# One pool for MLP and embedding, an early load of p, and w1's products sorted into high and low runs

## The chip, the cores and the metric
The kernel runs on one core of a Trainium2 chip. The metric is the device time of one execution in microseconds. Engines are named as the profile names them: PE is TensorE's matmul, PEld its weight load, DVE is VectorE, ACT is ScalarE, SP is SyncE, which issues most of the DMAs. L173 is line 173 of the kernel before.

## The reference
A trunk of two layers over 256 tokens of width 2048, in float32. Each layer adds three terms to h:

```
h += mixer(rmsnorm(h))                     # layer 0: RG-LRU; layer 1: 2-D neighbourhood attention
h += relu(rmsnorm(h) @ w1)^2 @ w2          # w1: 2048 x 8192, w2: 8192 x 2048
h += sigmoid(rmsnorm(h) @ Wg) * (p @ Wp)   # Wg: 2048 x 2048, p: 256 x 256, Wp: 256 x 2048
```

A last rmsnorm ends it. The third line is called the embedding here; Wg is `ple` and Wp is `proj` in the kernel.

## The kernel before
Every operand of a product is split into a high part, rounded to the format in which TensorE multiplies (fp32r), and a low part, the rest. A product is high x high + high x low + low x high, all summed in PSUM.

**Weights.** `block` (L93) loads 1 MB of weights into a buffer `raw` (SP, L98) and splits it in two halves: a cast to `wh` on ACT (L105) and a subtraction to `wl` on DVE (L106). A half is a step, and covers two rows of 128 inputs by 512 outputs. There are three raw buffers for the whole kernel and four `wh` and four `wl`; a stage may add raw buffers of its own from its pool (`phase`, L87): two in the MLP and two in the embedding, none in the mixers. The buffers are used in turn.

**Two ways to multiply.** `tproduct` (L136: w2, the output products, the gate) keeps the activations stationary and streams 512 columns of weights, eight matmuls with `wh` (L143, L144) and then four with `wl` (L148) for each step. `add` (L159: w1, and q and k of the attention) keeps a 128 x 128 piece of the weights stationary. For each of four output tiles and each of two rows it issues the high product with 512 columns (L173: the high and the low half of the activations side by side) and then the low product with 256 columns (L174), which is added to the second half of the same PSUM tile. A group is 8 steps x 4 tiles x 2 rows = 64 such pairs. The first two steps of a group are done first for tiles 0 and 1, then for tiles 2 and 3 (`held`, L176 to 187). In the mixer of layer 0, w_in goes through `product` (L189), three matmuls of 256 columns.

PSUM has three accumulators `mm` of two tiles each; a group of `add` takes two. `joined` (L201) adds the two halves of a PSUM tile: ACT copies the second half (L204), DVE adds (L206), after which the accumulator is free.

**MLP** (L581). It has a pool of its own, with the tile r2 (the squared norm factor) and the two raw buffers. For each quarter f: four groups of w1, each squared and split into activations, then four products with w2, each of eight steps and summed into h by `residual_add` (L339, L346 with r2 as the factor). In the last quarter the sum is followed by `settle` (L284): the squares of h on ACT (L222), then transposes and the split for the next stage.

**Embedding** (L612). A new pool, opened when the MLP's has been closed. `ple_load` loads p from ACT's queue (L608) and splits it (L198, L199) into `pls`. Then for each of four groups: twelve matmuls of p with proj (L636 to 638), and the gate, a product by `tproduct` of eight steps, with sigmoid and sum.

**Order.** The tile framework places instructions in each engine's queue by order of the program and by when it reckons them ready, and adds the waits. A tile of a new pool waits for the tiles of the closed pool whose place it takes. `self.later` holds small pieces of work that `tick` (L117) advances once after every step.

Of the kernel before, what the change touches and what calls it, by code (L numbers as in the profile page):

```python
# [19 lines left out]
P = 128  # L20
D = 2048
T = 256
# [8 lines left out]
V_MIX, V_MLP, V_PLE, V_FIN, V_CW, V_CB, V_AB, V_XB, V_LAM = 0, 2, 4, 6, 7, 11, 12, 14, 16  # L31
# [7 lines left out]
class Late:  # L39


    def __init__(self, tiles):
        self.tiles = tiles
# [8 lines left out]
class Trunk:  # L52
    def __init__(self, ctx, tc, d):
        self.tc, self.nc, self.d = tc, tc.nc, d
        nc = self.nc
        pool = lambda name, bufs, **kw: ctx.enter_context(tc.tile_pool(name=name, bufs=bufs, **kw))
        self.const = pool("const", 1)
        self.state = pool("state", 1)
        self.wraw = pool("wraw", 3)
        self.wsplit = pool("wsplit", 4)  # L60
        self.work = pool("work", 2)
        self.psum = pool("psum", 3, space=PSUM)
        self.psm = pool("psm", 2, space=PSUM)

        self.vec = self.const.tile([P, N_VEC * NC], F32, name="vec")
        self.ones = self.const.tile([P, P], F32, name="ones")
        self.ident = self.const.tile([P, P], F32, name="ident")
        nc.gpsimd.memset(self.ones, 1.0)
        make_identity(nc, self.ident)
        nc.scalar.dma_start(self.vec, d["vec"])  # L70
        self.later = []
        self.spare, self.turn = (None, 0), 2
        self.ahead = 0

    def v(self, which, c):
        i = which * NC + c
        return self.vec[:, i : i + 1]
# [81 lines left out]
    def add(self, ps, w, xs, quarters, before=None, loads=1, summed=False):  # L159
        nc = self.nc  # L160

        def tiles(step, ts):
            k0, wh, wl = step
            for t in ts:
                o = ps[t // 2][:, t % 2, :]
                c = slice(t * P, (t + 1) * P)
                for k in range(2):
                    kc = k0 + k
                    first, last = kc == 0, kc == len(xs) - 1
                    if summed:  # L170
                        self.product(o, wh[:, k, c], wl[:, k, c], xs[kc], first, last)
                    else:
                        nc.tensor.matmul(o, wh[:, k, c], xs[kc], start=first, stop=False)  # L173
                        nc.tensor.matmul(o[:, T:], wl[:, k, c], xs[kc][:, :T], start=False, stop=last)  # L174

        held = []  # L176
        for step in self.steps(w, quarters, loads):
            if before:
                before(step[0])
            if step[0] < 4:  # L180
                tiles(step, (0, 1))
                held.append(step)
                if len(held) == 2:
                    for s in held:
                        tiles(s, (2, 3))
            else:
                tiles(step, range(4))
# [390 lines left out]
        return out  # L578


    def mlp(self, layer, home, other):  # L581

        with self.phase("mlp", 2) as pool:
            self._mlp(pool, layer, home, other)

    def _mlp(self, pool, layer, home, other):
        nc = self.nc
        r2 = pool.tile([P, 2], F32, name="r2")
        self.norm_later(lambda r: nc.vector.tensor_tensor(r2, r, r, ALU.mult))
        xs = self.xlist(self.xs)  # L590
        for f in range(4):
            acts = []
            for g in range(4):
                ps = self.group(self.d["w1"][layer, 4 * f + g], xs)
                o = self.state.tile([P, 4, 512], F32R, name=f"{other}{g}")
                for i in range(2):
                    u = self.joined(ps[i], "u")
                    nc.vector.scalar_tensor_tensor(u, u, 0.0, u, ALU.max, ALU.mult)
                    self.split(o[:, 2 * i : 2 * i + 2, :], u)
                acts.append(o)  # L600
            w = lambda g: self.d["w2"][layer, g, 4 * f : 4 * f + 4]
            self.residual(w, self.xlist(acts), V_PLE + layer, home, by=r2, last=f == 3)


    def ple_load(self, pool, layer):
        nc = self.nc
        raw = pool.tile([P, 2, T], F32, name="p_raw")
        nc.scalar.dma_start(raw, self.d["p"][layer])  # L608
        self.pls = pool.tile([P, 2, 512], F32R, name="pls")
        self.split(self.pls, raw)  # L610

    def ple(self, layer, which, home):  # L612
        with self.phase("ple", 2) as pool:
            self.ple_load(pool, layer)
            self._ple(pool, layer, which, home)

    def _ple(self, pool, layer, which, home):
        nc = self.nc
        r = pool.tile([P, 2], F32, name="r_ple")
        self.norm_later(lambda tok: nc.vector.tensor_copy(r, tok))  # L620
        xs = self.xlist(self.xs)
        if which is not None:
            self.xs = self.new_xs(home)
        else:
            gain = pool.tile([P, D], F32, name="gain")
            nc.scalar.dma_start(gain, self.d["gain"])
        for g in range(NG):
            if g % 2 == 0:
                halves = self.block(self.d["proj"][layer, g // 2])
            wh, wl = (t.rearrange("p (k n) -> p k n", k=2) for t in next(halves))  # L630
            pj = pool.tile([P, 2, 512], F32, name="pj", bufs=2)
            pp = [self.psm.tile([P, 512], F32, name="pp", tag="psm") for _ in range(2)]
            for s in range(2):
                for k in range(2):
                    xh, xl = (self.pls[:, k, a + s * P : a + (s + 1) * P] for a in (0, T))
                    nc.tensor.matmul(pp[s], xh, wh[:, k, :], start=k == 0, stop=False)  # L636
                    nc.tensor.matmul(pp[s], xl, wh[:, k, :], start=False, stop=False)
                    nc.tensor.matmul(pp[s], xh, wl[:, k, :], start=False, stop=k == 1)
                nc.scalar.copy(pj[:, s, :], pp[s])
            ps = self.tgroup(self.d["ple"][layer, g], xs)  # L640
            if g == 0:
                self.norm_begin()
            for s in range(2):
                h = self.h[g][:, s, :]
                u = self.work.tile([P, 512], F32, name="u", tag="joined")
                nc.scalar.activation(u, ps[:, s, :], AF.Sigmoid, scale=r[:, s : s + 1])
                nc.vector.tensor_tensor(u, u, pj[:, s, :], ALU.mult)
                nc.vector.tensor_tensor(h, h, u, ALU.add)
                if which is None:
                    self.norm_square(g, s)  # L650
                    nc.vector.tensor_tensor(h, h, gain[:, 512 * g : 512 * (g + 1)], ALU.mult)
            if which is not None:
                self.settle(g, which, self.xs[g])
        if which is None:
            self.last()
# [15 lines left out]
    def run(self):  # L671
        self.load_h()
        self.rg_mixer()
        self.mlp(0, "xs", "as")
        self.ple(0, V_MIX + 1, "as")
        self.na_mixer()
        self.mlp(1, "as", "xs")
        self.ple(1, None, None)

# [79 lines left out]
```

## Time and profile before

| | us |
|---|---|
| median of 3 runs | 2383.24 |
| the three runs | 2381.78, 2383.24, 10307.08 |
| profiled execution | 2382.47 |
| its span | 2380.7 |
| PE busy | 2330.8 (98%) |
| PEld busy | 1996.5 (84%) |
| DVE busy | 1422.3 (60%) |
| ACT busy | 1177.4 (49%) |

The span is the time from the first to the last instruction of the profiled execution. Busy times of engines lie beside each other. A matmul's listed duration overlaps with the next matmul's; how fast TensorE works is read from the distance of the starts. The mean granted clock of TensorE is 0.993 of full speed. The chain that ended last runs over PE for 92% of the span. One of the three runs is far off the others; the profile agrees with those two.

### The profile page before, as it was taken

To read this page: it belongs to the slowest core of one execution; us is meant where nothing else is said; L and a number is where in the kernel's file an instruction comes from. 1 tells how busy PE (TensorE), PEld (TensorE's weight loads), DVE (VectorE), ACT (ScalarE), POOL (GpSimd) and SP (SyncE) were. 2 spreads that over 40 slices of the span, in tenths; PEclk is the share of its full clock that TensorE was granted. 3 is DMA by queue.
4 is the path that set the end of the run, shared out by engine and by line. 5 is a ranking of instruction groups with operands and counts; after the bars stand their busy time and mean duration, and the time that the engine had idled before them with its cause. 6 is when DMAs were issued, how large, how long until landed. Compare 5 with 4: busy or idle time off the path is not lost.

```text
span 2380.7 us, 30449 instructions
## 1 busy us (share of the span) xinstructions
PE 2330.8 (98%) x12356; PEld 1996.5 (84%) x12356; DVE 1422.3 (60%) x1634; ACT 1177.4 (49%) x1527; POOL 0.9 (0%) x9
## 2 busy tenths in 40 slices
PE   8999999999999999989999999999999999999897
PEld 8999888888888888868888888888888888888685
DVE  6878756556556556546576666555555555555464
ACT  7888544344344344445455455544344344344353
POOL 0000000000000000000000000000000000000000
PEclk9999999999999999999999999999999999999998
DMA  7454555555555555544555545555555555555452
GB/s 285 171 177 181 215 183 188 195 190 183 193 195 185 187 194 193 179 157 166 175 178 183 179 174 209 178 186 190 190 193 191 184 192 195 187 185 194 148 193 88
DMA packets 63947, 440.93 MB, mean 185 GB/s; under 512 B 6976, under 2 KB 7104, under 8 KB 11968
## 3 DMA queue, kind: packets, MB, share of 16 engines
q1 hardware_dynamic: 62112, 433.09, 51.2%
q10 hardware_dynamic: 1696, 5.92, 0.7%
q8 instruction: 96, 1.57, 0.3%
q14 instruction: 43, 0.35, 0.0%
HBM read 436.88 MB, written 2.10 MB: 184 GB/s over the span
## 4 chain that ended last, share of the span: by engine, by line
PE 92%; ACT 3%; DVE 3%; issue 1%; DMA 1%; SPq 0%; ACTq 0%
PE mm L173 25%; PE mm L143 16%; PE mm L144 16%; PE mm L148 16%; PE mm L174 13%; ACT wh L105 1%; PE mm L194 1%; DVE wl L106 1%; PE mm L192 1%; PE mm L193 1%; PE pt L281 1%; DVE ig L432 1%; ACT L211 1%; DMA p_raw<-in_p 1%; ACT m L211 1%
## 5 line engine op out<-in xcount | busy, mean ns | idle before, releaser
L106 DVE TENSOR_TENSOR wl<-raw,wh 128x1024 fp32r<-128x1024 f32 x816 | 997.2, 1224 | 794.9 <-ACT wh L105 793.0
L105 ACT CAST wh<-raw 128x1024 fp32r<-128x1024 f32 x816 | 855.4, 1050 | 1029.0 <-PE mm L144 514.7
L173 PE MATMUL mm<-as,wh 128*128 128x512 f32 x1536 | 543.6, 398 | 0.0
L174 PE MATMUL mm<-as,wl 128*128 128x256 f32 x1536 | 431.4, 281 | 0.0
L173 PE MATMUL mm<-xs,wh 128*128 128x512 f32 x1024 | 362.2, 399 | 0.0
L143 PE MATMUL mm<-wh,as 128*128 128x512 f32 x896 | 350.5, 391 | 0.0
L144 PE MATMUL mm<-wh,as 128*128 128x512 f32 x896 | 349.1, 390 | 0.0
L173 PEld LDWEIGHTS mm<-as,wh 128*128 128x128 f32 x1536 | 288.5, 188 | 70.4
L143 PE MATMUL mm<-wh,xs 128*128 128x512 f32 x768 | 301.0, 392 | 0.0
L144 PE MATMUL mm<-wh,xs 128*128 128x512 f32 x768 | 299.2, 390 | 0.0
L174 PEld LDWEIGHTS mm<-as,wl 128*128 128x128 f32 x1536 | 290.2, 189 | 0.4
L174 PE MATMUL mm<-xs,wl 128*128 128x256 f32 x1024 | 287.7, 281 | 0.0
L148 PE MATMUL mm<-wl,as 128*128 128x512 f32 x896 | 241.1, 389 | 0.0
L173 PEld LDWEIGHTS mm<-xs,wh 128*128 128x128 f32 x1024 | 192.4, 188 | 47.9
L148 PE MATMUL mm<-wl,xs 128*128 128x512 f32 x768 | 205.8, 389 | 0.0
L143 PEld LDWEIGHTS mm<-wh,as 128*128 128x128 f32 x896 | 168.4, 188 | 34.8
L144 PEld LDWEIGHTS mm<-wh,as 128*128 128x128 f32 x896 | 168.4, 188 | 34.2
L148 PEld LDWEIGHTS mm<-wl,as 128*128 128x128 f32 x896 | 167.6, 188 | 34.5
L174 PEld LDWEIGHTS mm<-xs,wl 128*128 128x128 f32 x1024 | 193.4, 189 | 0.2
L148 PEld LDWEIGHTS mm<-wl,xs 128*128 128x128 f32 x768 | 144.1, 188 | 30.2
L143 PEld LDWEIGHTS mm<-wh,xs 128*128 128x128 f32 x768 | 144.3, 188 | 29.6
L144 PEld LDWEIGHTS mm<-wh,xs 128*128 128x128 f32 x768 | 144.2, 188 | 29.4
(138 smaller groups left out, 1892.5 us busy)
## 6 DMA issues: line engine op xcount, KB each, us to landing
raw<-in_w SPq DMA_DIRECT2D x256, 1024.0 KB, 4.8
raw<-in_qkv SPq DMA_DIRECT2D x48, 1024.0 KB, 4.8
raw<-in_ple SPq DMA_DIRECT2D x32, 1024.0 KB, 4.8
raw<-in_w_in SPq DMA_DIRECT2D x28, 1024.0 KB, 4.8
raw<-in_w_out SPq DMA_DIRECT2D x16, 1024.0 KB, 4.8
raw<-in_na_out SPq DMA_DIRECT2D x16, 1024.0 KB, 4.7
raw<-in_w_in SPq DMA_DIRECT2D x8, 512.0 KB, 8.3
raw<-in_gates SPq DMA_DIRECT2D x4, 1024.0 KB, 4.8
```

Of the source, the lines that this page charges most:

```text
L105: nc.scalar.copy(wh, raw[:, c])
L106: nc.vector.tensor_tensor(wl, raw[:, c], wh.bitcast(F32), ALU.subtract)
L143: nc.tensor.matmul(ps[:, s, :], part(k, 0), wh[:, k, :], start=first and k == 0, stop=False)
L144: nc.tensor.matmul(ps[:, s, :], part(k, T), wh[:, k, :], start=False, stop=False)
L148: nc.tensor.matmul(ps[:, s, :], part(k, 0), wl[:, k, :], start=False, stop=last and k == n - 1)
L173: nc.tensor.matmul(o, wh[:, k, c], xs[kc], start=first, stop=False)
L174: nc.tensor.matmul(o[:, T:], wl[:, k, c], xs[kc][:, :T], start=False, stop=last)
L192: nc.tensor.matmul(o, a, x[:, :T], start=first, stop=False)
L193: nc.tensor.matmul(o, a, x[:, T:], start=False, stop=False)
L194: nc.tensor.matmul(o, b, x[:, :T], start=False, stop=last)
L211: self.tc.stamp_issue_order_token(self.nc.scalar.activation(*args, **kw).ins, "table")
L281: self.nc.tensor.transpose(pt[:, j, s * P : (s + 1) * P], self.h[g][:, s, c], self.ident)
```

## The change
`mlp_ple` opens one pool for both stages; the embedding's tiles and its raw buffers come from it, and the turn of the raw buffers goes on. `ple_load` is called as the MLP begins, loads p by SP's queue, and puts the split into `self.later`, to be done after 16 steps. `self.lows` is 1 in the MLP of layer 0, 2 in that of layer 1, and 0 elsewhere. With 1, `add` issues both high products of a tile in a step and then both low ones (runs of two). With 2, it issues all high products of a step's tiles and then all low ones (runs of eight, and of four in the first two steps of a group).

```diff
@@ def add
+        def lows(step, ts):
+            k0, wh, wl = step
+            for t in ts:
+                o = ps[t // 2][:, t % 2, :]
+                c = slice(t * P, (t + 1) * P)
+                for k in range(2):
+                    kc = k0 + k
+                    nc.tensor.matmul(o[:, T:], wl[:, k, c], xs[kc][:, :T], start=False, stop=kc == len(xs) - 1)
+
         def tiles(step, ts):
...
                     else:
                         nc.tensor.matmul(o, wh[:, k, c], xs[kc], start=first, stop=False)
-                        nc.tensor.matmul(o[:, T:], wl[:, k, c], xs[kc][:, :T], start=False, stop=last)
+                        if not self.lows:
+                            nc.tensor.matmul(o[:, T:], wl[:, k, c], xs[kc][:, :T], start=False, stop=last)
+                if self.lows == 1:
+                    lows(step, (t,))
+            if self.lows == 2:
+                lows(step, ts)
@@ mlp
-    def mlp(self, layer, home, other):
+    def mlp_ple(self, layer, home, other, which):
 
         with self.phase("mlp", 2) as pool:
-            self._mlp(pool, layer, home, other)
-
-    def _mlp(self, pool, layer, home, other):
+            self.mlp(pool, layer, home, other)
+            self.lows = 0
+            self.ple(pool, layer, which, other)
+
+    def mlp(self, pool, layer, home, other):
         nc = self.nc
         r2 = pool.tile([P, 2], F32, name="r2")
+        self.lows = 1 + layer
+        self.ple_load(pool, layer)
@@ ple_load
-        nc = self.nc
         raw = pool.tile([P, 2, T], F32, name="p_raw")
-        nc.scalar.dma_start(raw, self.d["p"][layer])
+        self.nc.sync.dma_start(raw, self.d["p"][layer])
         self.pls = pool.tile([P, 2, 512], F32R, name="pls")
-        self.split(self.pls, raw)
-
-    def ple(self, layer, which, home):
-        with self.phase("ple", 2) as pool:
-            self.ple_load(pool, layer)
-            self._ple(pool, layer, which, home)
-
-    def _ple(self, pool, layer, which, home):
+
+        def work():
+            for _ in range(16):
+                yield
+            self.split(self.pls, raw)
+
+        self.later.append(work())
+
+    def ple(self, pool, layer, which, home):
@@ run
-        self.mlp(0, "xs", "as")
-        self.ple(0, V_MIX + 1, "as")
+        self.mlp_ple(0, "xs", "as", V_MIX + 1)
         self.na_mixer()
-        self.mlp(1, "as", "xs")
-        self.ple(1, None, None)
+        self.mlp_ple(1, "as", "xs", None)
```

## Rows read from the trace of the kernel before

**Rows 1.** The page's first part: busy us (share of the span) xinstructions.
```profile
PE 2330.8 (98%) x12356; PEld 1996.5 (84%) x12356; DVE 1422.3 (60%) x1634; ACT 1177.4 (49%) x1527; POOL 0.9 (0%) x9
```

**Rows 2.** Chain of waits, first embedding's start: start us, us, what.
```profile
1031.52 0.76 DVE h L346
...
1033.07 6.16 DMA p_raw<-in_p
```

**Rows 3.** Timeline there: start us, us, engine, line, op, out<-in, xcount [idle before <-releaser].
```profile
1030.41 1.07 PE L148 MATMUL mm<-wl,as 128*128 128x512 f32 x4
...
1032.96 0.33 SPq L98 DMA_DIRECT2D raw<-in_proj  x1
...
1033.56 0.19 ACT L222 ACTIVATION_READ_ACCUMULATOR sq<-h 128x1 f32 x1
...
1040.87 0.79 PE L636 MATMUL pp<-wh,pls 128*128 128x512 f32 x1 [9.39 <-ACT wh L105]
...
1046.67 0.40 PE L144 MATMUL mm<-wh,xs 128*128 128x512 f32 x1
```

**Rows 4.** Timeline of the second embedding's start.
```profile
2251.60 1.07 PE L148 MATMUL mm<-wl,xs 128*128 128x512 f32 x4
...
2268.29 0.40 PE L144 MATMUL mm<-wh,as 128*128 128x512 f32 x1
```

**Rows 5.** Windows: from:to us, PE, PEld, DVE, ACT, POOL busy (x), PEclk, DMA share, GB/s.
```profile
1040.87:1046.28 5.41, 5.37 (x12) 3.78 (x13) 3.96 (x4) 3.51 (x4) 0.00 (x0) 0.50 0.15 27
```

**Rows 6.** Timeline of PE, second group of the first embedding.
```profile
1068.31 1.07 PE L148 MATMUL mm<-wl,xs 128*128 128x512 f32 x4
...
1072.25 0.39 PE L144 MATMUL mm<-wh,xs 128*128 128x512 f32 x1
```

**Rows 7.** Timeline, w1 of layer 0: first and last of 17 L173 in a row.
```profile
400.24 0.40 PE L173 MATMUL mm<-xs,wh 128*128 128x512 f32 x1
...
405.90 0.40 PE L173 MATMUL mm<-xs,wh 128*128 128x512 f32 x1
```

**Rows 8.** Timeline, w2: first and last of 37 matmuls of 512 columns.
```profile
1020.44 0.39 PE L143 MATMUL mm<-wh,as 128*128 128x512 f32 x1
...
1028.60 0.39 PE L143 MATMUL mm<-wh,as 128*128 128x512 f32 x1
```

**Rows 9.** Timeline of PE, w_in: first and last of 13 matmuls of 256 columns.
```profile
151.10 0.28 PE L192 MATMUL mm<-xs,wh 128*128 128x256 f32 x1
...
152.53 0.28 PE L192 MATMUL mm<-xs,wh 128*128 128x256 f32 x1
```

**Rows 10.** Timeline of PE where the size changes: mixer of layer 0, attention.
```profile
227.37 0.40 PE L143 MATMUL mm<-wh,as 128*128 128x512 f32 x1
...
228.76 0.39 PE L143 MATMUL mm<-wh,as 128*128 128x512 f32 x1
...
1195.23 0.28 PE L558 MATMUL ps<-qk,qk 128*128 128x256 f32 x1
...
1195.71 0.39 PE L143 MATMUL mm<-wh,as 128*128 128x512 f32 x1
```

**Rows 11.** Timeline of ACT where the MLP of layer 0 begins.
```profile
316.71 1.05 ACT L105 CAST wh<-raw 128x1024 fp32r<-128x1024 f32 x1 [1.67 <-PE mm L144]
318.34 0.63 ACT L222 ACTIVATE sq<-h 128x512 f32<-128x512 f32 x1 [0.58 <-DVE h L344]
```

**Rows 12.** Timelines of ACT and DVE at a group's end, w1 of layer 1.
```profile
1560.91 0.59 ACT L204 COPY low<-mm 128x512 f32<-128x512 f32 x1 [0.48 <-PE mm L174]
...
1561.61 0.69 DVE L206 TENSOR_TENSOR u<-mm,low 128x512 f32<-128x512 f32 x1
```

**Rows 13.** Timeline of SP in the attention's output product.
```profile
1452.28 0.80 SPq L98 DMA_DIRECT2D raw<-in_w  x2
1455.82 40.36 SPq L98 DMA_DIRECT2D raw<-in_na_out  x8
```

**Rows 14.** Lines by form, w_in: line, engine, op, shapes xcount | busy us, mean ns | idle before.
```profile
L194 PEld LDWEIGHTS mm<-xs,wl 128*128 128x128 f32 x512 | 98.5, 193 | 1.4 <-DVE wl L106 1.4
```

More of the change, by code (lines that the diff above doesn't have):

```diff
@@ L578, in na_probs @@
         return out
-    def mlp(self, layer, home, other):
+    def mlp_ple(self, layer, home, other, which):
         with self.phase("mlp", 2) as pool:
-            self._mlp(pool, layer, home, other)
-    def _mlp(self, pool, layer, home, other):
+            self.mlp(pool, layer, home, other)
+            self.lows = 0
+            self.ple(pool, layer, which, other)
+    def mlp(self, pool, layer, home, other):
         nc = self.nc
         r2 = pool.tile([P, 2], F32, name="r2")
+        self.lows = 1 + layer
+        self.ple_load(pool, layer)
         self.norm_later(lambda r: nc.vector.tensor_tensor(r2, r, r, ALU.mult))
```

## The prediction
> **What bounds the kernel now.** I read the page first: TensorE is busy 98% of the span [rows 1], so only two things can shorten this program: stretches where TensorE stands still, and the interval at which it issues matmuls. No other engine's time counts unless TensorE waits for it.
>
> Next the chain of waits, for the stretches where it leaves TensorE. Outside the first 250 us it does so for long only at the start of each embedding stage. There it runs from the last MLP sum (DVE, L346, at 1031.52) to the load of p, 6.16 us from 1033.07 [rows 2]. The timeline of that place shows why [rows 3]: SP issues proj's load at 1032.96, just after that sum, and p's load goes out with it; TensorE, idle for 9.39 us, starts L636 at 1040.87, released by the cast of proj's weights, which ACT does behind the cast of p. Both loads go into tiles of a pool that opens when the MLP's pool closes, and r2, which the last sum reads, lives in the MLP's pool. The second embedding looks the same [rows 4]. The clock completes the picture: the twelve proj matmuls after the idle run at a granted 0.50, that is 1.2 GHz [rows 5].
>
> Last the timeline of TensorE alone, for the interval of the matmuls that w1 issues, and of uniform streams of 512 and 256 columns.
>
> **Edit 1: one pool for MLP and embedding; p loaded and split as the MLP begins.** What it removes: the p load, the pls split and the opening of a pool from the way between MLP and embedding. I measure the loss from the four last lows (x4) of a stage to the second gate matmul (L144), which spans the idle, the proj matmuls and the slow clock. Warm, at the second group of the same embedding, that takes 1072.25 - 1068.31 = 3.94 us [rows 6]. First embedding: 1046.67 - 1030.41 = 16.26, a loss of 12.32 [rows 3]. Second: 2268.29 - 2251.60 = 16.69, a loss of 12.75 [rows 4]. Together **25.07 us**.
>
> What is late next there: proj's cast (ACT) and its low half (DVE). proj's load becomes one more turn of the five weight buffers, so SP issues it while w2 still runs. Whether the cast also stands before the squares of the last sum on ACT, or behind them, no row of this place shows. The nearest is the other stage boundary: when the MLP follows the mixer, ACT casts weights at 316.71 and squares h at 318.34 [rows 11], and TensorE has no gap. I take that order and cost it at nothing; the bound the other way is rival C. The squares and the reciprocal root, which today fall into the idle time, then run beside matmuls; ACT is about half busy there, and their result is wanted only at the first sigmoid, a group (some 25 us) later.
>
> What it adds: at the start of the MLP one issue on SP, ahead of w1's first loads (0.33 us by the proj issue in [rows 3]; a quarter of a weight block's bytes), and after 16 steps one cast and one subtraction on ACT and DVE, each smaller than the weight casts that these engines do beside every step. In layer 1, w1's first two loads were issued at 1452.28, with eight loads of the attention's output product still to come behind them [rows 13]: the p load joins them, with those eight blocks of TensorE's work as its cover. Price 0; if the old pool kept it waiting, w2's and w1's loads behind it on SP would be late too. I bound that by what the same kind of wait costs today, 12.3 us a layer.
>
> **Edit 2: order in w1.** Every product stays: 1024 pairs (high 512 columns, low 256) in each layer, 2048 in all. Today high and low alternate: from 400.24 to 405.90 are 16 pairs, 353.8 ns a pair [rows 7]. In uniform streams with a weight load for each matmul, 512 columns take (1028.60 - 1020.44)/36 = 226.7 ns [rows 8] and 256 take (152.53 - 151.10)/12 = 119.2 ns [rows 9], together 345.9. So an alternating pair pays 7.9 ns for its change of size and back. No row shows runs of 2 or 8. Bounds:
> - Best: the change costs nothing in short runs. In the attention four 256s between 512s take 1195.71 - 1195.23 = 480 ns, 120 each [rows 10]. Then all 2048 x 7.9 = 16.2 us come back.
> - Worst: each return to 512 costs what it does after the mixer's long 256 stream, where six intervals take 228.76 - 227.37 = 1.39 us instead of 1.36 [rows 10], 30 ns. Layer 0 has 512 runs of two pairs (2 x 7.9 - 30 = -14 ns each): 7.3 us lost. Layer 1 has, per group, six runs of eight (33 ns gained) and four of four (2 ns): 16 x 0.206 = 3.3 gained. Net 4 us lost.
> - Taken: each run pays one change at the alternating price, so n pairs save (n - 1) x 7.9. Layer 0: 512 x 7.9 = 4.0. Layer 1: 16 groups x (6 x 7 + 4 x 3) x 7.9 = 6.8. Together **10.9 us**. I take this because the runs are nearer in length to the attention's four than to the mixer's long stream.
>
> [...]
>
> PSUM in layer 1: three accumulators, two per group. The first two tiles are now finished before the other two begin their last step: the copy of their low part starts at 1560.91 and the sum that frees the buffer ends at 1562.30 [rows 12], about when the group ends (half a step, 4 pairs or 1.4 us, after 1560.9). The next group wants that buffer 8 pairs, 2.8 us, later. With the lows last, the tiles are finished 4 lows (0.48 us) before the end instead of 1.4, so 0.9 of the 2.8 us of slack goes. Costed at 0.
>
> **Sum.** The profiled execution took 2382.47 us (span 2380.7), 0.8 below the median of the runs, 2383.24. 2382.47 - 25.07 - 10.9 = 2346.5; I say **2347 us**, 1.5% below the median.
>
> **Rivals.**
> - B, the order in w1 is worth nothing: 2382.47 - 25.07 = 2357.4. For it: no row shows these short runs, and after the mixer's stream six 512s in a row still average 232 ns [rows 10]. [...] Against: uniform streams are clearly tighter. Within the bounds above it runs from 2353 to 2361.
> - C, ACT squares the last sum before it casts proj. Then TensorE waits for sum and squares (to 1033.75, the last entry before the proj matmuls in [rows 3]), then a cast of 1.05: L636 at about 1034.9, a gap of 3.4 us, plus at most 2.8 for a slow clock: 3.4 to 6.2 each, total 2353 to 2359. Against: [rows 11]. For: proj's cast never ran ahead here before.
> - D, the freed slack in PSUM isn't enough: if ACT and DVE do a weight split (1.05 and 1.23 us) before the copy and the sum, the buffer comes about when it is wanted, up to 1 us late at 16 boundaries: up to 2363.
> - E, slower: weight loads become the bound in runs of lows. A load shows 193 ns [rows 14], and a 256-column matmul streams in 119. Today every low's load lies under a 512. If a load in a run took its full 193 ns, each low after a low would take 74 ns more: 512 in layer 0 and 16 x 54 = 864 in layer 1, 1376 x 74 = 102 us; 2382.47 - 25 + 102 = 2459. It beats edit 1 from 18 ns a load on. Against it almost decisively: the mixer's 256 stream has just such loads and runs at 119.
> - F, the pool is shared but the embedding still waits (proj's load still late, or the p load holds SP at the MLP's start): the 25 us stay or come back elsewhere, 2372.
>
> **How the numbers follow.** Forecast 0.56, B 0.21, C 0.09, D 0.06, F 0.05, E 0.03. The best bound of edit 2 reaches 2341; B, C and D reach 2361 to 2363. Range **2339 to 2362**, which leaves out F, E and the tails. Two per cent of the median is 47.7 us (about what a measurement of this kernel can tell from no change): faster means under 2335.6, which needs more than both edits at their best (41 us), 0.04. Slower is E, 0.03. Within 2%: 0.93.
>
> **What would show it.** Right: no TensorE idle of microseconds at the two embedding starts; the proj matmuls there at half the interval that [rows 5] gives, with the clock at 1.00; L144 about 4 us after the last four lows; p's load on SP near w1's first; a w1 group (64 pairs, now 22.6 us) shorter by some 0.25 us in layer 0 and 0.43 in layer 1. Wrong: highs in w1 still at 235 ns or more after a high (B); a gap of 3 to 4 us with sq before wh (C); TensorE idle at a group's third tile, released by DVE (D); lows at 190 ns (E).

## The result, and the profile after

The changed kernel takes 2348.12 us (median; 2347.99 to 2348.41) against 2383.4 of the kernel before: ratio 0.9854, 95% interval 0.9835 to 0.9874. The prediction was 2347 with a range of 2339 to 2362. The profiled execution took 2348.25 us, 34.2 less than the 2382.47 of before.

The first part of the page of the profile:

```profile
PE 2315.7 (99%) x12356; PEld 1991.8 (85%) x12356; DVE 1420.1 (61%) x1634; ACT 1177.4 (50%) x1527; POOL 0.9 (0%) x9
```

The same instructions, in 34 us less. The timeline of PE at the two embedding starts answers [rows 3] and [rows 4]:

```profile
1024.91 1.07 PE L149 MATMUL mm<-wl,as 128*128 128x512 f32 x4
1025.82 0.39 PE L655 MATMUL pp<-wh,pls 128*128 128x512 f32 x1
...
1028.86 0.39 PE L145 MATMUL mm<-wh,xs 128*128 128x512 f32 x1
...
2229.85 1.07 PE L149 MATMUL mm<-wl,xs 128*128 128x512 f32 x4
2230.76 0.39 PE L655 MATMUL pp<-wh,pls 128*128 128x512 f32 x1
...
2233.80 0.39 PE L145 MATMUL mm<-wh,as 128*128 128x512 f32 x1
```

From the last four lows to the second gate matmul it is now 3.95 us in both, the warm value of [rows 6]: 16.26 - 3.95 = 12.31 and 16.69 - 3.95 = 12.74 have gone, 25.05 together. The windows over the proj matmuls show the clock that [rows 5] had at 0.50 (columns as there):

```profile
1025.82:1028.63 2.81, 2.81 (x13) 2.26 (x12) 2.54 (x3) 2.17 (x6) 0.00 (x0) 1.00 0.89 338
2230.76:2233.56 2.80, 2.80 (x13) 2.25 (x12) 2.54 (x3) 2.15 (x6) 0.00 (x0) 1.00 0.88 325
```

The rest is in w1. A stretch of w1 is four groups, 256 pairs. The windows run from its first matmul to the start of its last low, 0.12 us before the first matmul of w2. Windows over the first two stretches of each layer (the third and fourth repeat the second), before:

```profile
317.41:408.61 91.20, 91.20 (x521) 79.13 (x520) 54.67 (x65) 43.90 (x55) 0.00 (x0) 1.00 0.51 182
495.83:586.15 90.32, 90.32 (x512) 78.28 (x511) 51.95 (x53) 39.50 (x45) 0.00 (x0) 1.00 0.52 183
1538.70:1629.85 91.15, 91.15 (x521) 79.17 (x519) 54.67 (x65) 43.82 (x55) 0.00 (x0) 1.00 0.51 182
1717.02:1807.35 90.33, 90.33 (x513) 78.36 (x512) 51.96 (x53) 39.50 (x45) 0.00 (x0) 1.00 0.51 183
```

and after:

```profile
317.08:407.05 89.97, 89.97 (x521) 78.62 (x520) 54.80 (x65) 43.79 (x55) 0.00 (x0) 1.00 0.53 184
494.21:583.26 89.05, 89.05 (x512) 77.71 (x511) 52.10 (x53) 39.52 (x45) 0.00 (x0) 1.00 0.53 186
1520.76:1610.97 90.21, 90.21 (x520) 79.36 (x519) 53.95 (x64) 43.74 (x55) 0.00 (x0) 1.00 0.53 187
1698.16:1787.51 89.35, 89.35 (x512) 78.48 (x511) 51.33 (x52) 39.47 (x45) 0.00 (x0) 1.00 0.54 189
```

Layer 0, with runs of two, gains 1.23 + 3 x 1.27 = 5.0 us; layer 1, with runs of eight, 0.94 + 3 x 0.98 = 3.9. Together 8.9, and 25.05 + 8.9 = 34.0 of the 34.2 us. TensorE is busy throughout each of these windows, before and after: what differs is the interval of the matmuls, not a wait.

### The profile page after: what moved, and what is told of

The parts are those of the page before. It is cut to its first block, busy times and chain, and to the rows that moved or that the text cites. A ratio compares the mean times of both kernels' runs of the same rounds, so it can differ in the third digit from the quotient of the medians.

```text
span 2346.2 us, 30442 instructions
## 1 busy us (share of the span) xinstructions
PE 2315.7 (99%) x12356; PEld 1991.8 (85%) x12356; DVE 1420.1 (61%) x1634; ACT 1177.4 (50%) x1527; POOL 0.9 (0%) x9
## 4 chain that ended last, share of the span: by engine, by line
PE 93%; ACT 3%; DVE 3%; issue 1%; DMA 0%; SPq 0%; ACTq 0%
PE mm L183 25%; PE mm L144 16%; PE mm L145 16%; PE mm L149 16%; PE mm L170 10%; PE mm L185 3%; ACT wh L106 1%; PE mm L209 1%; PE mm L207 1%; PE mm L208 1%; DVE wl L107 1%; PE pt L296 1%; DVE ig L447 1%; ACT L226 1%; ACT m L226 1%
## 5 line engine op out<-in xcount | busy, mean ns | idle before, releaser
L183 PE MATMUL mm<-as,wh 128*128 128x512 f32 x1536 | 444.0, 395 | 0.0
L183 PEld LDWEIGHTS mm<-as,wh 128*128 128x128 f32 x1536 | 278.3, 189 | 53.7
L183 PE MATMUL mm<-xs,wh 128*128 128x512 f32 x1024 | 322.1, 396 | 0.0
L170 PE MATMUL mm<-xs,wl 128*128 128x256 f32 x1024 | 201.2, 278 | 0.0
L183 PEld LDWEIGHTS mm<-xs,wh 128*128 128x128 f32 x1024 | 156.3, 189 | 0.3
L170 PEld LDWEIGHTS mm<-as,wl 128*128 128x128 f32 x1024 | 144.0, 190 | 12.9
L207 PE MATMUL mm<-xs,wh 128*128 128x256 f32 x512 | 146.1, 286 | 8.3 <-ACT wh L106 7.3
```

Source lines behind the costliest of these rows:

```text
L207: nc.tensor.matmul(o, a, x[:, :T], start=first, stop=False)
```

## The experiments

Each edit is told against the changed kernel unless it says otherwise; the numbers of runs with an interval are ratios to the kernel before.

**The two edits by themselves.** e1 leaves w1 as it was:

```diff
-        self.lows = 1 + layer
+        self.lows = 0
```

> The change without its new order in w1 (high and low alternate as before). Theory: the two edits add up, and the pool edit is worth the two embedding starts, 25.1 us: 2357 to 2358 us, no idle of TensorE at either start. Rival (the new order gave more, through its earlier release of weight buffers): under 15 us of gain, above 2368.

Measured 2357.16 us, 0.9892 (0.9877 to 0.9907). e2 is the kernel before with the new `lows` and nothing else:

```diff
+            self.lows = 1 + layer
             self._mlp(pool, layer, home, other)
+            self.lows = 0
```

> The kernel before with only the new order in w1. Theory: 9 us, by the lengths of the eight w1 stretches in the trace after (5.1 in layer 0, 3.9 in layer 1): 2373 to 2374 us, with the two idle stretches of 9.4 us still there. Rival (the order is worth nothing by itself): 2382 to 2384.

Measured 2373.37 us, 0.9959 (0.9945 to 0.9973); the second stretch of w1 again lasts 89.05 us, and TensorE again stands still for 9.48 us at the first embedding. So the edits add up: by the medians e1 gains 26.5 us and e2 10.3, 36.8 together, where both edits gave 35.3; the traces give them 25.05 and 8.9.

**What of the pool edit counts.** e3 keeps the shared pool, but loads and splits p where the embedding begins, from ACT's queue (w1 alternates here and in e4):

```diff
-        self.nc.sync.dma_start(raw, self.d["p"][layer])
+        self.nc.scalar.dma_start(raw, self.d["p"][layer])
...
-        self.later.append(work())
+        self.split(self.pls, raw)
```

> One pool for MLP and embedding, but p is loaded by ACT's queue and split where the embedding begins, as before; w1 alternates. Theory: what cost the time is that tiles of the embedding waited for the closed pool; with a place of its own the p load can go out before the last sum, so 2357 to 2360 us. Rival: the load of p itself is the cost wherever it stands behind the squares on ACT; then TensorE waits 6.2 us for the transfer and 2 us for the split and the cast at both starts, and the time stays at 2378 to 2383.

Measured 2356.58 us (one run), as fast as e1. The timeline of ACT shows how far "late" moved:

```profile
258.73 0.36 ACTq L625 DMA_DIRECT2D p_raw<-in_p  x1
...
267.45 0.62 ACT L213 CAST pls<-p_raw 128x512 fp32r<-128x512 f32 x1 [7.26 <-DMA p_raw<-in_p]
```

Written at the embedding's start, the load was issued 770 us earlier, in the mixer, and the split with it. The likely reason, which no run separates, is that p now had a place that nothing else used. So e3 shows that it doesn't matter where the load is written; a load that goes out late in a shared pool was not run. e4 does the opposite: p early in a small pool of its own, the two stages with a pool each.

```diff
+        with self.tc.tile_pool(name="early", bufs=1) as early:
+            self.ple_load(early, layer)
+            with self.phase("mlp", 2) as pool:
+                self.mlp(pool, layer, home, other)
+            with self.phase("ple", 2) as pool:
+                self.ple(pool, layer, which, other)
```

> p is loaded and split early into a pool of its own, but the embedding still opens its own pool when the MLP's closes; w1 alternates. Theory: proj's load still waits for the last sum (1032.96), lands 4.8 us later and is cast in 1.05 us, so TensorE is idle for about 7.4 us instead of 9.4 and the clock still falls: 2376 to 2380 us. Rival (the load of p was the whole wait): 2357 to 2360.

Measured 2379.33 us (one run). The chain of waits of e4 at the first embedding, and two pieces of the chain at the second:

```profile
1031.32 1.42 DVE h L361 x2
1032.75 4.75 DMA raw<-in_proj
1037.60 1.05 ACT wh L106
1038.70 0.79 PE pp L656
...
2251.57 6.34 DMA raw<-in_proj
...
2259.08 0.79 PE pp L656
```

proj's load alone keeps TensorE waiting for 7.4 us at the first start and for 9.0 at the second, where the load takes longer. p's load was only the longer of two waits for the same thing, the closing of the MLP's pool. From the last four lows to the second gate matmul it takes 13.65 and 15.93 us in e4, so an early p by itself gives 2.6 us at the first start and 0.8 at the second, of the 12.3 and 12.7 that go with the shared pool. The sharing is what counts.

**Length of the runs or layer?** e5 has runs of eight in both layers (`self.lows = 2`).

> As the change, but runs of eight in both layers. Theory (the length of the runs decides, not the layer): layer 0 then gains 3.9 us like layer 1 instead of 5.1, 2349.3 us, and its w1 stretches become 89.35 us like those of layer 1. Rival (the layer's tiles decide): layer 0 stays at 89.05 a stretch, 2348.1.

Measured 2349.58 us, 0.9859 (0.9842 to 0.9875); the second stretch of layer 0, and that of e9 below:

```profile
495.31:584.66 89.35, 89.35 (x512) 78.48 (x511) 51.35 (x52) 39.47 (x45) 0.00 (x0) 1.00 0.54 189
```

```profile
494.40:583.52 89.12, 89.12 (x512) 78.53 (x511) 49.44 (x52) 41.03 (x46) 0.00 (x0) 1.00 0.54 189
```

89.35, as in layer 1: the length decides. e9 keeps back the lows of two steps, for runs of sixteen:

```diff
                 tiles(step, range(4))
+                if self.lows == 3:
+                    pend.append(step)
+                    if len(pend) == 2:
+                        for s in pend:
+                            lows(s, range(4))
+                        pend.clear()
```

> As the change, but in w1 of both layers the lows of two steps are kept back and issued together: runs of sixteen (of four in the first two steps of a group, as with runs of eight). Theory A (the return from lows to highs costs some 28 ns once a run is long enough, as after the mixer's long stream): a group has three returns fewer than with runs of eight, 84 ns, so a stretch of w1 goes from 89.35 to 89.0 us and the whole from 2349.6 to 2346.9 us. Theory B (the cost of a return grows with the run's length): no gain, 89.35 a stretch, 2349.6 us.

Measured 2348.64 us, 0.9856 (0.984 to 0.9872), 89.12 a stretch: 0.23 less, two thirds of what A said and not the nothing of B; the whole lies between the two. The 12 returns that a stretch has fewer give some 20 ns net each: in w1 a return after sixteen lows costs about what one after eight does.

e6 has runs of two in w1 of both layers and also in q and k of the attention.

> As the change, but runs of two wherever high and low have different widths: w1 of both layers, and q and k of the attention. Theory: layer 1's w1 goes from 89.35 to 89.05 us a stretch (1.2 us in all) and each of the eight groups of q and k, 64 pairs at 4.9 ns, gives 0.31 us (2.5 in all): 2344.4 us. Rival (the layer decides): no gain in w1 of layer 1, 2345.6.

Measured 2345.47 us, 0.9842 (0.9827 to 0.9857): the fastest of all, 2.6 us under the changed kernel by the medians, though the two intervals overlap. In the profiles w1 of layer 1 goes to 89.05 as expected, and q and k from 48.37 to 47.77 us in three of four stretches. The first of the four gained nothing; the reason turned up below.

**Is it the change of size?** In e7 w1's lows stream 512 columns too, so that all matmuls are equal; the edit also reached q and k of the attention, which the expectation forgot (8 groups x 64 pairs x 100 ns = 51 us more).

```diff
-                            nc.tensor.matmul(o[:, T:], wl[:, k, c], xs[kc][:, :T], start=False, stop=last)
+                            nc.tensor.matmul(o, wl[:, k, c], xs[kc], start=False, stop=last)
```

> As the change, but w1 alternates and its low products also stream 512 columns (they add low times low as well, which the other kernels leave out). Every matmul of w1 then has 512 columns. Theory (the change of size is the cost): 226.7 ns each, so a stretch of w1 lasts 512 x 0.2267 = 116 us and the whole 2357.2 + 2048 x (453.4 - 353.0) ns = 2563 us. Rival (the alternation between the high and the low weights is the cost, at any size): 233 ns or more each, a stretch of 119 us, 2576 us or more.

Measured 2614.55 us; 2614.55 - 51 is 2563. High and low weights alternate as before, now at 601.30 - 599.94 = 1.36 us for six, 227 ns each:

```profile
599.94 0.39 PE L185 MATMUL mm<-xs,wl 128*128 128x512 f32 x1
...
601.30 0.39 PE L185 MATMUL mm<-xs,wl 128*128 128x512 f32 x1
```

In e8 each high product is two of 256 columns (q and k again included):

```diff
-                        nc.tensor.matmul(o, wh[:, k, c], xs[kc], start=first, stop=False)
+                        nc.tensor.matmul(o[:, :T], wh[:, k, c], xs[kc][:, :T], start=first, stop=False)
+                        nc.tensor.matmul(o[:, T:], wh[:, k, c], xs[kc][:, T:], start=False, stop=False)
```

> As the change, but w1 alternates and each high product is issued as two of 256 columns, with a weight load of its own: three equal matmuls for each pair. Theory (equal sizes run at the uniform price): 3 x 119.2 = 357.6 ns a pair instead of 353.0, 2357.2 + 9.4 = 2366.6 us. Rival (w1's operands make a matmul dearer at any size): above 360 ns a pair, 2372 us or more.

Measured 2375.9 us (one run), which by the total is the rival's number. But q and k, which neither figure counted, take 4.2 us more than in e1, so without them some 2371.7 are left. And 16 triples take 565.88 - 560.12 = 5.76 us, 360 ns each where the theory had 357.6 and the rival more than 360. A matmul comes every 120 ns, within 1 ns of the uniform 119.2, so the theory holds to that accuracy, but e8 alone does not decide:

```profile
560.12 0.28 PE L184 MATMUL mm<-xs,wh 128*128 128x256 f32 x1
...
565.88 0.28 PE L184 MATMUL mm<-xs,wh 128*128 128x256 f32 x1
```

e7 seemed to settle it: a change of size costs. But the first group of the attention, where e6 had gained nothing, alternates in the kernel before as w1 does, and does so without the price. Sixteen pairs there take 1185.81 - 1180.26 = 5.55 us, 347 ns, against the 354 of [rows 7]:

```profile
1161.11 0.59 PE L246 MATMUL mb<-n_diag,ones 128*128 128x256 f32 x2
...
1180.26 0.39 PE L173 MATMUL mm<-as,wh 128*128 128x512 f32 x1
...
1185.81 0.39 PE L173 MATMUL mm<-as,wh 128*128 128x512 f32 x1
```

The fast pairs begin right behind a matmul of another kind (L246, full float32, run as two); the six pairs before it took 353 ns on average. e10 puts one such matmul, whose output nobody reads, into each stretch of w1 of the kernel of e1:

```diff
+            if self.kick and step[0] == 4:
+                self.kick = False
+                pb = self.psm.tile([P, 512], F32, name="kb", tag="psm")[:, :T]
+                nc.tensor.matmul(pb, self.ones, self.vec[:, :T], start=True, stop=True)
```

> The shared pool with w1 alternating as before (2357.2 us), and once in each of the eight w1 stretches, after its second step, one full-precision matmul of 256 columns whose output nobody reads, like the one (L246 of the kernel before) after which the first group of the attention alternated at 346.7 ns a pair instead of 353.3. Theory A (alternating sizes cost nothing by themselves; it is a state into which the stream falls where it starts, and such a matmul lifts it out): 240 pairs of a stretch gain 6.6 ns each, less 0.43 us for the matmul, so a stretch goes from 90.33 to some 89.2 us and the whole to 2348 us. Theory B (each change of size has its price, and the attention's group is fast for another reason): 0.43 us more in each stretch, 2360 to 2361 us.

Measured 2357.99 us, 0.9897 (0.9881 to 0.9914), because two things happened: the first stretch of each layer fell to 347 ns a pair and stayed there to its end, the other six stayed at 353. e11 and e12 put the same matmul one and two pairs later in the step (condition `2 * t + k == 0`, and `== 1`, behind the low product).

> As e10, with the extra matmul one pair later in the step. In e10 the two first stretches of w1 in each layer fell to 346.7 ns a pair and stayed there, the six others stayed at 353.8. Theory A (where in the slow pattern of three pairs the extra matmul falls decides): one of the two places, one or two pairs later, turns the six slow stretches into fast ones of about 89.2 us. Theory B (the transposes that stood before it in the two first stretches are needed): the six stay at 90.76 us in both runs.

> As e10, with the extra matmul two pairs later in the step. Theory A: if one pair later does not do it, this does, 89.2 us in the six later stretches. Theory B: the six stay at 90.76 us.

Measured 2349.64 and 2351.96 us (one run each). In both, all six later stretches are now fast: 89.16 us in e11 and 89.18 in e12 for 90.76 in e10. The same stretch in e10 and in e11:

```profile
495.33:586.09 90.76, 90.76 (x515) 78.74 (x513) 51.93 (x53) 39.50 (x45) 0.00 (x0) 1.00 0.52 183
```

```profile
494.47:583.63 89.16, 89.16 (x514) 77.92 (x513) 51.88 (x53) 39.48 (x45) 0.00 (x0) 1.00 0.52 186
```

and 16 pairs in it, 525.78 - 520.13 = 5.65 us in e10, 525.50 - 519.96 = 5.54 in e11:

```profile
520.13 0.40 PE L184 MATMUL mm<-xs,wh 128*128 128x512 f32 x1
...
525.78 0.40 PE L184 MATMUL mm<-xs,wh 128*128 128x512 f32 x1
```

```profile
500.46 0.59 PE L190 MATMUL kb<-vec,ones 128*128 128x256 f32 x2
...
519.96 0.40 PE L184 MATMUL mm<-xs,wh 128*128 128x512 f32 x1
...
525.50 0.40 PE L184 MATMUL mm<-xs,wh 128*128 128x512 f32 x1
```

So the same alternating stream runs at either of two intervals, and which one is set by where it was last interrupted: theory A. The kernels of e10 and e11 issue the same matmuls, with one of them a pair later in each stretch. That transposes must stand before is excluded (B), since these six have none. The first stretches, which have, were slow at the end in e12 (both) and in layer 1 in e11. The transposes too can move the stream: in e11's layer 1 the seven pairs from 1524.62 to 1527.05 us, behind the first transposes, take 347 ns each, and those behind the later transposes and the extra matmul 353. As a version it isn't worth having: the extra matmul costs some 0.4 us a stretch, and e6 is faster.

## Why the prediction was right

**Edit 1, 25.07 us predicted, 25.05 measured.** The loss was read off as the difference to a warm pass through the same code, idle and slow clock included, and e1 gives it alone. Rival C was decided as forecast. The proj matmuls start at 1025.82, before the first squares of the last sum, and before the cast of 1025.11 has ended, so proj's own cast is an earlier one still:

```profile
1025.11 1.05 ACT L106 CAST wh<-raw 128x1024 fp32r<-128x1024 f32 x1 [1.67 <-PE mm L145]
1026.81 0.63 ACT L237 ACTIVATE sq<-h 128x512 f32<-128x512 f32 x1 [0.65 <-DVE h L361]
```

What was wrong there is a detail: the split was expected 16 steps into the MLP. In both layers it stands before w1 begins, as in e3; in the changed kernel ACT waits for p in the mixer:

```profile
266.05 0.62 ACT L213 CAST pls<-p_raw 128x512 fp32r<-128x512 f32 x1 [5.94 <-DMA p_raw<-in_p]
```

TensorE has no wait there, and w1 of layer 0 begins at 317.08 where it began at 317.41 before. The price of 0 held; the reason given for it (the split hides beside the steps of w1) didn't.

**Edit 2, 10.9 predicted, 8.9 measured: the mis-sized term.** Its step was "each run pays one change at the alternating price", which gave 4.0 us for layer 0 and 6.8 for layer 1. Measured were 5.0 and 3.9, the other way round. That the sum missed by only 2.0 is in part luck: the errors, 1.0 too little and 2.9 too much, offset each other in part. Runs of eight pay close to the bound called worst. In the timeline of layer 1:

```profile
1560.76 2.00 PE L183 MATMUL mm<-as,wh 128*128 128x512 f32 x8
1562.60 1.11 PE L170 MATMUL mm<-as,wl 128*128 128x256 f32 x8
1563.55 2.00 PE L183 MATMUL mm<-as,wh 128*128 128x512 f32 x8
```

eight highs take 1.84 us instead of the 1.81 of [rows 8], eight lows 0.95 as in [rows 9]: about the 30 ns that [rows 10] showed after the long stream. Runs of two pay far less a return:

```profile
360.48 0.63 PE L183 MATMUL mm<-xs,wh 128*128 128x512 f32 x2
360.95 0.39 PE L170 MATMUL mm<-xs,wl 128*128 128x256 f32 x2
361.18 0.63 PE L183 MATMUL mm<-xs,wh 128*128 128x512 f32 x2
```

0.70 us for two pairs (0.697 by the whole stretch, 89.05 us and its last low), where two alternating ones took 0.707 and uniform ones would take 0.692.

The prediction had gone by the attention's four matmuls of 256 columns, as nearest in length. They indeed leave no mark on what follows: eight of 512 columns behind them take 1197.52 - 1195.71 = 1.81 us, the uniform price. A line a little further on in the timeline of [rows 10]:

```profile
1197.52 0.84 PE L148 MATMUL mm<-wl,as 128*128 128x512 f32 x3
```

w1's own runs of four do pay: four highs take 1544.90 - 1543.97 = 0.93 us instead of 0.91 (rows below). So the length of a run alone doesn't set the price, and a row of other operands was the wrong measure for w1. And the 7.9 ns themselves were no price of a change of size: e10 to e12 show the alternating stream all but without them. The prediction took one stretch of alternation for all; the rows that would have warned it, at 1180 us, are in the trace of before.

**The rivals.** B (the order is worth nothing) falls with e2. E falls with the rows above: lows in a run come every 119 ns, not every 193. F falls with e1. D was nearer than forecast. At a group's end in layer 1 ACT and DVE did put the weight split first, as D had it; PE, ACT and DVE there:

```profile
1543.97 1.09 PE L183 MATMUL mm<-as,wh 128*128 128x512 f32 x4
1544.90 0.63 PE L170 MATMUL mm<-as,wl 128*128 128x256 f32 x4
...
1546.78 1.09 PE L183 MATMUL mm<-as,wh 128*128 128x512 f32 x4
```

```profile
1543.22 1.05 ACT L106 CAST wh<-raw 128x1024 fp32r<-128x1024 f32 x1 [1.74 <-PE mm L183]
1544.17 1.07 ACT L219 COPY low<-mm 128x512 f32<-128x512 f32 x2
```

```profile
1544.30 1.22 DVE L107 TENSOR_TENSOR wl<-raw,wh 128x1024 fp32r<-128x1024 f32 x1 [1.57 <-ACT wh L106]
1545.44 1.28 DVE L221 TENSOR_TENSOR u<-mm,low 128x512 f32<-128x512 f32 x2
```

The first of the two sums ends about half way through their 1.28 us, at 1546.1, and the third tile of the next group starts at 1546.78: 0.7 us of slack are left of 2.8, not the 1.9 that the prediction kept. TensorE didn't wait.

## What to carry to other kernels

Price a stall by the same code run warm elsewhere in the same trace, from a matmul before it to one behind it, so that idle time and slow clock come out together; and ask which tile's place is waited for, since the load on the chain (p) may be only the longer of two that wait for the same pool. Where an interval between matmuls is a term of the sum, read it in every stretch that has the pattern: a stretch that differs for no visible reason is the experiment already done. An order that is worth a few nanoseconds a matmul is best tried at its shortest length first; here runs of two beat runs of eight.

## What the runs showed of the hardware

The same alternating stream of 512 and 256 columns ran at 353 or at 347 ns a pair, at a granted clock of 1.00 both times, and without an interruption kept its interval to the end of the stretch. It could be moved from the one to the other by a single foreign matmul, but only at some places of the stream. Read one by one in the traces, the pairs of the slow case take some 361, 349 and 350 ns in turn; those of the fast case 343 and 350 in turn (e11) or 347 each (e12, and at 1180 us before). At 347 a pair costs about the sum of the uniform intervals (226.7 + 119.2 = 345.9, [rows 8, 9]).

The Trainium skill ("TensorE: Matmul & The Clock Gate", section "Back-to-back issue gap") gives an isolated warm matmul its columns over 2.4 GHz plus about 2.5 ns, and says that a stream with weight loads is paced by both, at about 131 ns a matmul of 512 columns. The runs here, streams with a weight load for each matmul, agree with neither: 226.7 ns at 512 columns, where the formula, as an estimate, has 216; and one and the same alternating pair at 353 or 347, which no formula in a matmul's own columns can give.

What inside TensorE holds the stream in the one pattern or the other, and why a return in w1 costs some 20 to 30 ns after eight lows, only some 5 after two, and nothing behind the attention's four, no run here shows.
